# Reordering the products of the seven-product couples, scaling C by rs squared, and other fills around the inverse, in a one-core Hymba block

## The chip, the core and the metric

The kernel runs on one core of a Trainium2 chip. The metric is the device time of one execution in microseconds (us); the median of the runs is compared. Five engines work beside each other and meet at semaphores: PE (TensorE), DVE (VectorE), ACT (ScalarE), POOL (GpSimd), and SP, which here only issues transfers. Each engine takes its instructions in the order of the program.

## What is computed

One layer of a hybrid block over 528 tokens (16 meta tokens and 512 real ones), width 2048:

```
hn = rmsnorm(h_res, norm_in_g)
P  = hn @ w_in                      # 2048 x 8320: lora, r, k, v, g (RWKV-7), B, C, h, gate (short conv)
r, k, v, g, wl, al = token_shift(P[:, :4224])
...                                 # decay and a from two low-rank paths, kk normalised per head
S_t = S_{t-1} diag(w_t) - (S_{t-1} kk_t)(kk_t a_t)^T + v_t k_t^T ;  y_t = S_t r_t   # 16 heads of 64
y_a = (groupnorm(y) + bonus) * silu(g)
y_b = B * conv3(C * h) * silu(g_c)
out = rmsnorm(h_res + concat(y_a, y_b) @ w_out)[16:]
```

All products are fp32-exact: each operand is split into a high and a low fp32r part, and a product is three matmuls (high x high, high x low, low x high).

## The kernel before, in words

The recurrence is done in chunks of 64 tokens: for each of eight pairs of heads `prepare(i)` builds decays, the small Gram products (`gram`) and a 16-wide inverse by DVE; for each two pairs `invert` widens it to 64 by small products `t`, `z` on PE; then `recur` goes through nine chunks for all heads, and the output projection follows (products M, P, Q with seven products in the place of eight).

**The flow.** The input projection is a generator of PE matmuls, `mains()`. Seven column tiles go singly; the other 58 go in 29 couples, numbered here from 0, `couple(p)`, each (t0, t1) one pair of 128-column tiles. A couple takes four of the sixteen 128-row blocks of the input with a second four and the two token halves in a Strassen-like form with seven block products in place of eight; the other eight blocks go straight ("plain", the function `rest`). With 12 matmuls in a form and 24 in a rest, a couple is 7 x 12 + 4 x 24 = 180 matmuls. They gather in four PSUM banks: za, zb, ze, zd (tiles `psa_`, `psb_`, `pse_`, `psd_`, named after t0). za and ze are used several times: ACT copies an interim value (`keep`, L617) or DVE adds it (`add`, L613) before PE goes on adding into the bank.

**The order on PE is written by hand** (`manual_schedule` for PE). All other work on PE, that is the Gram products, the inverse and the recurrence, is placed between matmuls of the flow: `fill(ns)` runs the flow for so many nanoseconds, by 0.46 ns for each column, before the next small product. The table `FW` holds these lengths. The order on DVE, ACT, POOL and SP is set by a scheduler from priorities; `ahead()` gives high priority.

**The weights of a couple.** `sums_of(p + 1)` issues the two loads `ra`, `rb` for couple p + 1 from within couple p, and makes from them on ACT, DVE and POOL the operands of the seven forms: `ah`, `al` (W11, W21), `m` (T1), `bh`, `bl` (T2, W22), `ch`, `cl` (T3, T4). `plain_of(p + 1, 1)` loads `rp` for t1 and splits it: `ph` on ACT, then `pl` on POOL; `plain_of(p, 0)` does so for t0 (`pl` on DVE). All these blocks (128 x 1024) share nine places in SBUF: a block can be written only when the last reader of the block that had its place is done, and a load that must wait for that waits at the head of SP's queue. In the built program the place of `pl` for t1 is that of `ah` of the same couple in most couples (21 of couples 1 to 28), and the place of the raw load `rp` for t1 is that of the couple's own `ah` in 6 couples (3, 9, 13, 14, 19, 20), of `ra` in 14, of `rb` in 6, and of the earlier couple's last `pl` in 2. `bl` follows the earlier couple's `ph` for t1 in 27 of 28.

**h and C.** In the couples (h, C) C is the t1 tile. Both are multiplied by the token scale rs on DVE, then POOL multiplies them (`q_h_C`, L423), ACT and DVE make the convolution `cv`.

Of the kernel before, what the change touches and what calls it, by code (L numbers as in the profile page):

```python
# [13 lines left out]
ALU = mybir.AluOpType  # L14
# [8 lines left out]
META = 16  # L23
L = SEQ + META
# [16 lines left out]


FW = dict(
    evac=34, start=1062, lora=2200, gram=8000, gram_b=13500, gram2=5500, misc=2000, v=2000, vt=1000, solve=24500, solve_first=30000,
    tr=3200, lev=3000, cp=4200, out=1500, begin=20800, p=2900, u=2900, s=4800, last=3700, mix=2600,
)


# [2 lines left out]
W0 = META + HS  # L51
# [32 lines left out]
def hymba_kernel(ctx: ExitStack, tc: tile.TileContext, xt, xtok, front, w_in, w_out, pv, lup, cst, msk, gf, out):  # L84
    nc = tc.nc
# [169 lines left out]
    o = 0  # L255
# [145 lines left out]
    got = {}  # L401

    def use(what, i, q):
        if what == "lora":
            use_lora(q)
        elif what in ("k", "v"):
            t = cq.tile([P, LP], F32, tag=what, name=f"{what}{i}")
            nc.gpsimd.memset(t[:, META:CH], 0.0)
            shifted(q, tile_of[what] + i, t[:, CH:LP], t[:, 0:META])
            got[what, i] = t  # L410
        elif what in ("r", "g"):
            pool, tag = (cq, f"r{i % 2}") if what == "r" else ((cq, "g"), (tp, "cw"))[i % 2]
            t = pool.tile([P, SEQ], F32, tag=tag, name=f"{what}{i}")
            shifted(q, tile_of[what] + i, t)
            if what == "g":
                gate(t, t, f"r{i}")
                later((14000, 8000)[i % 2], lambda: nc.sync.dma_start(gated[i], t))
            got[what, i] = t
        elif what == "C":
            got[what, i] = q  # L420
        elif what == "h":
            u = got["C", i][:, META - 2 : L]
            nc.gpsimd.tensor_tensor(out=u, in0=u, in1=q[:, META - 2 : L], op=ALU.mult)  # L423
            cv = tp.tile([P, SEQ], F32, tag="cw", name=f"cv{i}")
            nc.scalar.activation(cv, u[:, 0:SEQ], AF.Copy, scale=col(V_CW, i))
            for j in (1, 2):
                nc.vector.scalar_tensor_tensor(
                    out=cv, in0=u[:, j : SEQ + j], scalar=col(V_CW, 8 * j + i), in1=cv, op0=ALU.mult, op1=ALU.add
                )
            got[what, i] = cv  # L430
            if i == 0:
                bg = tm("bg")[:, 0:SEQ]
                nc.sync.dma_start(bg, bgd)
                nc.gpsimd.tensor_tensor(out=cv, in0=cv, in1=bg, op=ALU.mult)
                later(9000, lambda: nc.sync.dma_start(mixd[NPAIR], cv))
        elif what == "B":
            b = q[:, META:L]
            if i == 0:
                got[what, i] = tp.tile([P, SEQ], F32, tag="cw", name="cw0")
                nc.scalar.copy(got[what, i], b)  # L440
            else:
                cv = got["h", i]
                o = direct.get(NPAIR + i, cv)
                nc.gpsimd.tensor_tensor(out=o, in0=cv, in1=b, op=ALU.mult)
                if o is cv:
                    later(9000, lambda: nc.sync.dma_start(mixd[NPAIR + i], cv))
        else:
            g = q[:, META:L]
            gate(g, g, f"c{i}")
            cv = got["h", i] if i else got["B", 0]  # L450
            nc.vector.scalar_tensor_tensor(out=cv, in0=cv, scalar=0.5, in1=g, op0=ALU.mult, op1=ALU.mult)
            if i == 0:
                later(5000, lambda: nc.sync.dma_start(bgd, cv))
        ready.add((what, i))
# [118 lines left out]
    def couple(p):  # L573
# [7 lines left out]
        def bank(name):  # L581
            return pm.tile([P, W0], F32, tag="main", name=f"ps{name}_{names[0]}")
# [25 lines left out]
        def part(n, t, c):  # L608
            return qq[:, n, (c, W0)[t] : (W0, L)[t]]

        def add(o, x, z, c):
            with ahead():
                nc.vector.tensor_tensor(out=o, in0=z[:, c:W0], in1=x, op=ALU.add)  # L613

        def keep(o, z, c):
            with ahead():
                nc.scalar.copy(o, z[:, c:W0])  # L617
# [11 lines left out]
        ze = bank("e")  # L629
        yield from form(ze, S1, "T1", META, True)  # L630
        keep(part(0, 1, META), ze, META)
        yield from form(za, S2, "T2", c0)
        keep(part(1, 0, f1), za, f1)
        yield from form(ze, S4, "W22", f1, False, False)
        if p + 1 < len(couples):
            sums_of(p + 1)
        elif chain:
            split_chain()
        yield from form(za, S3, "T3", META)
        add(part(1, 1, META), part(0, 1, META), za, META)  # L640
        yield from rest(ze, 1, 0)
        add(part(1, 0, f1), part(1, 0, f1), ze, f1)
        yield from form(za, X22, "T4", META, False, False)
        zd = bank("d")
        yield from rest(zd, 1, 1, True)
        add(part(1, 1, META), part(1, 1, META), zd, META)
        with ahead():
            q = qq[:, 1, f1:L]
# [2 lines left out]
        if p + 1 < len(couples):  # L651
            plain_of(p + 1, 1)
        yield from rest(zb, 0, 0)
        add(part(0, 0, f0), part(0, 0, f0), zb, f0)
        yield from rest(za, 0, 1)
        with ahead():
            q = qq[:, 0, f0:W0]
            nc.vector.tensor_tensor(out=q, in0=q, in1=rs[:, f0:W0], op=ALU.mult)
            nc.vector.tensor_tensor(out=qq[:, 0, W0:L], in0=za[:, META:W0], in1=rs[:, W0:L], op=ALU.mult)
# [74 lines left out]
    def fill(ns):  # L734
        while ns > 0:
            seen = len(ready)
            t = step()
            if t is None:
                return
            ns -= t  # L740
            if len(ready) > seen:
                ns += FW["evac"]
# [23 lines left out]
    def ahead():  # L766
        return tc.high_priority(offset=AHEAD)
# [262 lines left out]
    def invert(two):  # L1030
# [10 lines left out]
        with ahead():  # L1041
            for q in both:
                nc.vector.transpose(xn[q][:, CH:LP], two[q]["xT"][:, 1:NCH].rearrange("p c s -> p (c s)"))
        fill(FW["tr"])
        z = [pz.tile([P, 2, 4, CH], F32, tag="tz", name=f"t{first}_{e}") for e in range(2)]
        for q in both:
            for k in range(4):
# [519 lines left out]
    z = {}  # L1567
# [159 lines left out]
```

## Time and profile before

| | |
|---|---|
| median of 3 runs | 1140.29 us (1137.03 to 1141.22) |
| the profiled execution | 1144.66 us, of which the span from first to last instruction is 1142.9 us |
| PE busy | 1020.0 us, 89% of the span |
| DVE, ACT, POOL busy | 868.8, 487.8, 265.1 us |
| mean granted TensorE clock | 0.958 |
| matmuls | 9535 |

PE is the engine with the least idle time. Its couples run from 104 us to 971 us of the span, the output projection after that. In the profile's rows a time in brackets is the idle time of the engine ahead of an instruction, and the arrow names what ended it.

### The profile page before, as it was taken

Reading aid. Unit: us, or ns where it says so; the run is one execution under the profiler, and the core shown is the slowest. Engines: PE = TensorE matmul, PEld = TensorE weight load, DVE = VectorE, ACT = ScalarE, POOL = GpSimd, SP = SyncE. Lnnn points to the kernel's source line nnn. Section 1 sums busy time; section 2 is a strip of 40 time slices with the busy share of each in tenths; the row PEclk is TensorE's granted clock in tenths of the full one; section 3 lists DMA queues with packets and bytes.
Section 4 is the critical chain, followed back from the end, with each engine's and each line's share of the span. In section 5 each row is a group of like instructions: output and inputs, shape, how many; then the busy total and the mean of one; then the engine's idle time right before and its main releaser. Section 6 shows DMA issues by size and latency. Waiting matters only on the chain. (4 is left out here: it accounts for less than half of the span.)

```text
span 1142.9 us, 23275 instructions
## 1 busy us (share of the span) xinstructions
PE 1020.0 (89%) x9535; PEld 951.0 (83%) x9535; DVE 868.8 (76%) x1355; ACT 487.8 (43%) x840; POOL 265.1 (23%) x211
## 2 busy tenths in 40 slices
PE   9998889788989878897989897998999898899997
PEld 8897879678979878897988897997898798788886
DVE  7699866558887668976687876657776689999895
ACT  8454433144543344542353443233333333655554
POOL 0122212113312221422232312222222322201101
PEclk9999989888999989999999899999999899999999
DMA  9323626523657322657323566486767376978653
GB/s 305 112 74 94 161 57 175 127 75 99 170 133 185 104 78 80 167 133 193 103 99 94 145 165 166 125 307 226 249 215 223 84 203 200 270 223 257 150 127 147
DMA packets 185563, 180.05 MB, mean 158 GB/s; under 512 B 112240, under 2 KB 141936, under 8 KB 185072
## 3 DMA queue, kind: packets, MB, share of 16 engines
q1 hardware_dynamic: 182864, 169.64, 50.2%
q0 software_dynamic: 2304, 8.39, 4.4%
q8 instruction: 75, 1.23, 0.4%
q10 hardware_dynamic: 288, 0.52, 0.1%
q14 instruction: 32, 0.26, 0.1%
HBM read 139.54 MB, written 38.97 MB: 156 GB/s over the span
## 5 line engine op out<-in xcount | busy, mean ns | idle before, releaser
L556 POOL TENSOR_TENSOR cl<-ra,ch 128x1024 fp32r<-128x1024 f32 x29 | 75.7, 2609 | 299.6 <-ACT ch L554 149.3
L568 ACT CAST ph<-rp 128x1024 fp32r<-128x1024 f32 x58 | 60.6, 1049 | 72.8 <-DMA rp<-in_w_in_dram 72.4
L570 POOL TENSOR_TENSOR pl<-rp,ph 128x1024 fp32r<-128x1024 f32 x29 | 70.8, 2443 | 58.6 <-ACT ph L568 48.1
L570 DVE TENSOR_TENSOR pl<-rp,ph 128x1024 fp32r<-128x1024 f32 x29 | 35.3, 1218 | 30.9 <-ACT ph L568 22.2
L545 ACT CAST m<-rb 128x512 fp32r<-128x512 f32 x29 | 18.0, 621 | 88.5 <-DVE rb L544 61.2
L542 ACT CAST ah<-ra 128x1024 fp32r<-128x1024 f32 x29 | 30.3, 1046 | 47.2 <-DMA ra<-in_w_in_dram 38.0
L1410 ACT CAST o<-x 128x512 fp32r<-128x512 f32 x56 | 34.0, 620 | 31.7 <-PE M L1438 12.9
L1438 PE MATMUL M<-o,S 128*128 128x512 f32 x192 | 46.1, 396 | 0.0
L548 ACT CAST bh<-rb 128x1024 fp32r<-128x1024 f32 x29 | 30.5, 1051 | 32.7 <-DVE rb L547 31.1
L1397 POOL DMA_DIRECT2D x<-in_w_out_dram x16 | 14.3, 895 | 125.9 <-DVE o L1411 100.9
L1438 PEld LDWEIGHTS M<-o,S 128*128 128x128 f32 x192 | 36.1, 188 | 8.7
L1411 DVE TENSOR_TENSOR o<-x,o 128x512 fp32r<-128x512 f32 x56 | 36.6, 685 | 5.6 <-ACT o L1410 4.9
L543 DVE TENSOR_TENSOR al<-ra,ah 128x1024 fp32r<-128x1024 f32 x29 | 35.2, 1215 | 7.1 <-ACT ah L542 7.1
L554 ACT CAST ch<-ra 128x1024 fp32r<-128x1024 f32 x29 | 30.4, 1049 | 15.4 <-DVE ra L549 11.5
L549 DVE TENSOR_TENSOR ra<-ra,rb 128x1024 f32<-128x1024 f32 x29 | 35.7, 1232 | 0.5
L553 DVE TENSOR_TENSOR bl<-rb,bh 128x1024 fp32r<-128x1024 f32 x29 | 35.3, 1216 | 0.1
L1410 ACT CAST o<-wo 128x512 fp32r<-128x512 f32 x42 | 25.0, 620 | 21.6 <-PE M L1438 8.0
L1438 PE MATMUL M<-o,m 128*128 128x512 f32 x108 | 27.3, 411 | 3.6 <-ACT o L1410 2.2
L1411 DVE TENSOR_TENSOR o<-wo,o 128x512 fp32r<-128x512 f32 x42 | 27.6, 686 | 2.4 <-ACT o L1410 2.1
L1438 PEld LDWEIGHTS M<-o,m 128*128 128x128 f32 x108 | 21.3, 198 | 9.0 <-ACT o L1410 2.6
L876 DVE TENSOR_TENSOR gt<-g,gmt 128x512 f32<-128x512 f32 (+1 forms) x48 | 23.9, 546 | 6.3 <-PE g L866 6.2
L546 DVE TENSOR_TENSOR m<-rb,m 128x512 fp32r<-128x512 f32 x29 | 19.9, 685 | 9.6 <-ACT m L545 9.4
(732 smaller groups left out, 4160.0 us busy)
## 6 DMA issues: line engine op xcount, KB each, us to landing
rp<-in_w_in_dram SPq DMA_DIRECT2D x58, 512.0 KB
ct<-opd SPq DMA_DIRECT2D x56, 320.0 KB
ra<-in_w_in_dram SPq DMA_DIRECT2D x29, 512.0 KB
rb<-in_w_in_dram SPq DMA_DIRECT2D x29, 512.0 KB
wo<-in_w_out_dram SPq DMA_DIRECT2D x21, 512.0 KB
opd<-gt SPq DMA_DIRECT2D x16, 576.0 KB
x<-in_w_out_dram POOLq DMA_DIRECT2D x16, 512.0 KB, 5.8
wr<-in_w_in_dram SPq DMA_DIRECT2D x10, 512.0 KB
```

Source lines behind the costliest of these rows:

```text
L542: nc.scalar.copy(ah, a)
L543: nc.vector.tensor_tensor(out=al, in0=a, in1=ah.bitcast(F32), op=ALU.subtract)
L548: nc.scalar.copy(bh, b)
L549: nc.vector.tensor_tensor(out=two, in0=two, in1=b[:, 0:H].unsqueeze(1).to_broadcast([P, 2, H]), op=ALU.subtract)
L553: nc.vector.tensor_tensor(out=bl, in0=b, in1=bh.bitcast(F32), op=ALU.subtract)
L554: nc.scalar.copy(ch, a)
L556: nc.gpsimd.tensor_tensor(out=cl, in0=a, in1=ch.bitcast(F32), op=ALU.subtract)
L568: nc.scalar.copy(h, r)
L570: (nc.gpsimd if n else nc.vector).tensor_tensor(out=lo, in0=r, in1=h.bitcast(F32), op=ALU.subtract)
L1410: nc.scalar.copy(hi, rq)
L1411: nc.vector.tensor_tensor(out=lo, in0=rq, in1=hi.bitcast(F32), op=ALU.subtract)
L1438: nc.tensor.matmul(bank[s], left(prod, jj, m, s), w, start=(jj == 0 and n == 0), stop=(jj == 7 and n == 2))
```

## The change

It does four things. The order of the products in a couple becomes W11, W21, T1, the rest of zd, T2, W22, the rest of ze, T3, the rest of zb, T4, the rest of za; it was W11, W21, T1, T2, W22, T3, the rest of ze, T4, the rest of zd, the rest of zb, the rest of za. `sums_of(p + 1)` stands ahead of W22 (behind it before), and `plain_of(p + 1, 1)` stands behind the add of zd, as before, which is now behind T3. For h, rs multiplies C on POOL (so that C carries rs squared), and h is taken without rs: DVE multiplies it into C, the second token half straight from PSUM. The add of zb gets high priority. And eight entries of `FW` change, one of them new.

```diff
-    ... gram2=5500, misc=2000, v=2000, vt=1000, solve=24500, solve_first=30000,
-    tr=3200, lev=3000, cp=4200, out=1500, ...
+    ... gram2=6500, misc=1500, v=1500, vt=500, solve=24000, solve_first=29500,
+    tr=3200, tr0=6500, lev=3000, cp=4200, out=3000, ...
...
         elif what == "h":
-            u = got["C", i][:, META - 2 : L]
-            nc.gpsimd.tensor_tensor(out=u, in0=u, in1=q[:, META - 2 : L], op=ALU.mult)
+            q, z = q
+            u = got["C", i]
+            nc.gpsimd.tensor_tensor(out=u[:, META - 2 : L], in0=u[:, META - 2 : L], in1=rs[:, META - 2 : L], op=ALU.mult)
+            with ahead():
+                for o, x in ((slice(META - 2, W0), q[:, META - 2 : W0]), (slice(W0, L), z[:, META:W0])):
+                    nc.vector.tensor_tensor(out=u[:, o], in0=u[:, o], in1=x, op=ALU.mult)
...
         ze = bank("e")
         yield from form(ze, S1, "T1", META, True)
         keep(part(0, 1, META), ze, META)
+        zd = bank("d")
+        yield from rest(zd, 1, 1, True)
         yield from form(za, S2, "T2", c0)
         keep(part(1, 0, f1), za, f1)
-        yield from form(ze, S4, "W22", f1, False, False)
         if p + 1 < len(couples):
             sums_of(p + 1)
...
+        yield from form(ze, S4, "W22", f1, False, False)
+        yield from rest(ze, 1, 0)
+        add(part(1, 0, f1), part(1, 0, f1), ze, f1)
         yield from form(za, S3, "T3", META)
         add(part(1, 1, META), part(0, 1, META), za, META)
-        yield from rest(ze, 1, 0)
-        add(part(1, 0, f1), part(1, 0, f1), ze, f1)
-        yield from form(za, X22, "T4", META, False, False)
-        zd = bank("d")
-        yield from rest(zd, 1, 1, True)
         add(part(1, 1, META), part(1, 1, META), zd, META)
...
             plain_of(p + 1, 1)
         yield from rest(zb, 0, 0)
-        add(part(0, 0, f0), part(0, 0, f0), zb, f0)
+        raw0 = t0[0] == "h"
+        with ahead():
+            add(part(0, 0, f0), part(0, 0, f0), zb, f0)
+        yield from form(za, X22, "T4", META, False, False)
         yield from rest(za, 0, 1)
+        if raw0:
+            use(*t0, (qq[:, 0], za))
+            return
...
-        fill(FW["tr"])
+        fill(FW["tr0"])
```

The last lines are in `invert`, ahead of the first products t. The numbers and shapes of the instructions stay the same on every engine; only their order, their operands in the h step, and the places of the weight blocks change.

On PE, in couple 13 (h2 and C2), the first row of each form or rest, before (T4, which reads like T3, stands between the rest of ze and the rest of zd). `psa` to `psd` are the banks za to zd, `ph_1` and `ph_0` the plain weights of t1 and t0:

```order
L589 MATMUL psa_h_5607<-xh,ah_5346 128x258
L589 MATMUL psb_h_5621<-xh,ah_5346 128x258
L589 MATMUL pse_h_5640<-s_114,m_5348 128x256
L589 MATMUL psa_h_5607<-xs_116,bh_5349 128x258
L589 MATMUL pse_h_5640<-xs_116,bh_5349 128x258
L589 MATMUL psa_h_5607<-xh,ch_5350 128x256
L589 MATMUL pse_h_5640<-xh,ph_1_5542 128x258
L589 MATMUL psd_h_5767<-xh,ph_1_5542 128x256
L589 MATMUL psb_h_5621<-xh,ph_0_5636 128x258
L589 MATMUL psa_h_5607<-xh,ph_0_5636 128x256
```

The same now:

```order
L594 MATMUL psa_h_5604<-xh,ah_5358 128x258
L594 MATMUL psb_h_5621<-xh,ah_5358 128x258
L594 MATMUL pse_h_5640<-s_114,m_5360 128x256
L594 MATMUL psd_h_5654<-xh,ph_1_5463 128x256
L594 MATMUL psa_h_5604<-xs_116,bh_5361 128x258
L594 MATMUL pse_h_5640<-xs_116,bh_5361 128x258
L594 MATMUL pse_h_5640<-xh,ph_1_5463 128x258
L594 MATMUL psa_h_5604<-xh,ch_5362 128x256
L594 MATMUL psb_h_5621<-xh,ph_0_5636 128x258
L594 MATMUL psa_h_5604<-xh,ph_0_5636 128x256
```

The first use of `ph_1` has moved from behind six forms to behind three.

On SP, around the load `rp_1` for couple 13, before (`sx`, `xT`, `xo`, `sn`, `sg`, `nd` are transfers of the inverse):

```order
L139 DMA rb_5343<-in_w_in_dram 128x1024
L1002 DMA sx_135<-y_4940 72x16x16
L804 DMA sn_5495<-n_5452 2x9x64
L993 DMA xT_4965<-sx_135 64x9x64
L994 DMA xo_4966<-sx_135 64x4x64
L804 DMA sg_5494<-ga_5372 64x9x64 x2
L804 DMA nd_5500<-sn_5495 72x16
L139 DMA rp_1_5540<-in_w_in_dram 128x1024
L804 DMA d_5499<-sg_5494 72x16x16
```

And now:

```order
L139 DMA rb_5355<-in_w_in_dram 128x1024
L810 DMA opd_74<-vs_5065 32x9x32
L786 DMA lur_6911<-in_lup_dram 128x256
L139 DMA rp_1_5461<-in_w_in_dram 128x1024
L1012 DMA sx_135<-y_5000 72x16x16
L814 DMA sn_5551<-n_5508 2x9x64
L1003 DMA xT_5025<-sx_135 64x9x64
L1004 DMA xo_5026<-sx_135 64x4x64
L814 DMA sg_5550<-ga_5409 64x9x64 x2
```

The load `rp_1` stands ahead of the inverse's transfers now; in both programs it takes the place of the couple's own `ah`.

On PE, in couple 14, around the first products `t` of the third inverse, before:

```order
L589 MATMUL psb_B_5885<-xh,ah_5690 128x256
L589 MATMUL pse_B_5904<-s_114,m_5692 128x256
L1050 MATMUL t_0_5916<-xn_5875,ga_4791 64x64 x2
L1050 MATMUL t_0_5916<-xn_5876,ga_5372 64x64 x2
L589 MATMUL psa_B_5867<-xs_116,bh_5693 128x256
```

And now:

```order
L594 MATMUL psb_B_5881<-xh,ah_5698 128x256
L594 MATMUL pse_B_5900<-s_114,m_5700 128x256
L594 MATMUL psd_B_5918<-xh,ph_1_5779 128x256
L594 MATMUL psa_B_5862<-xs_116,bh_5701 128x256
L594 MATMUL pse_B_5900<-xs_116,bh_5701 128x256
L594 MATMUL pse_B_5900<-xh,ph_1_5779 128x256
L1060 MATMUL t_0_5996<-xn_5911,ga_4853 64x64 x2
L1060 MATMUL t_0_5996<-xn_5912,ga_5409 64x64 x2
```

The products `t` stand behind the rests of zd and most of ze, where they stood in T1. In the second inverse they stand in T2 of couple 9, in the fourth in the rest of zd of couple 20.

The places of the blocks, in the built program now: the raw load `rp` for t1 takes the place of the couple's own `ah` in 8 couples (3, 4, 8, 9, 13, 15, 20, 28), of `ra` in 9 (5, 6, 12, 17, 18, 21, 22, 23, 26), of `rb` in 9 and of the earlier couple's last `pl` in 2 (1, 19). In couples 7, 14 and 16 (among those with `rb`) `ph` takes the place of `ah`. `pl` for t1 takes that of `ah` or `al` in 20. `bl` follows the earlier couple's `ch`, which T4 reads last, in all 28.

More of the change, by code (lines that the diff above doesn't have):

```diff
@@ L43 @@
 FW = dict(
-    evac=34, start=1062, lora=2200, gram=8000, gram_b=13500, gram2=5500, misc=2000, v=2000, vt=1000, solve=24500, solve_first=30000,
-    tr=3200, lev=3000, cp=4200, out=1500, begin=20800, p=2900, u=2900, s=4800, last=3700, mix=2600,
+    evac=34, start=1062, lora=2200, gram=8000, gram_b=13500, gram2=6500, misc=1500, v=1500, vt=500, solve=24000, solve_first=29500,
+    tr=3200, tr0=6500, lev=3000, cp=4200, out=3000, begin=20800, p=2900, u=2900, s=4800, last=3700, mix=2600,
 )
@@ L421, in use @@
         elif what == "h":
-            u = got["C", i][:, META - 2 : L]
-            nc.gpsimd.tensor_tensor(out=u, in0=u, in1=q[:, META - 2 : L], op=ALU.mult)
+            q, z = q
[4 more added lines that the diff above has]
+                    nc.vector.tensor_tensor(out=u[:, o], in0=u[:, o], in1=x, op=ALU.mult)
+            u = u[:, META - 2 : L]
             cv = tp.tile([P, SEQ], F32, tag="cw", name=f"cv{i}")
```

## The prediction

> **What bounds the kernel now.** I read the page's busy rows first, then the clock of the core.
>
> ```profile
> PE 1020.0 (89%) x9535; PEld 951.0 (83%) x9535; DVE 868.8 (76%) x1355; ACT 487.8 (43%) x840; POOL 265.1 (23%) x211
> PEclk9999989888999989999999899999999899999999
> core 0: 1142.9 us, clock 0.958
> ```
>
> PE sets the time: it idles 11% of the span, and the work of PE is not changed. So the question is which idle times go and which come. The mean clock of 0.958 means 2 x 0.042 x 1142.9 = 96 us at half clock, some 48 us of lost cycles: the second thing that can move.
>
> Next the waits of PE, by what ended them (us in total, times, longest):
>
> ```profile
> PE t L1050 <- DVE xn L1043: 15.4, 4, 4.6
> PE tz L754 <- DVE xT L1115: 7.2, 2, 4.6
> PE g L904 <- DVE gt L876: 7.1, 5, 4.2
> PE pse_k L589 <- ACT q_k_v L617: 4.5, 3, 2.4
> ...
> PE psa_v L589 <- DVE q_v_r L613: 3.8, 1, 3.8
> ...
> PE pse_h L589 <- POOL pl L570: 3.2, 3, 1.5
> ...
> PE psa_v L589 <- ACT q_v_r L617: 0.4, 1, 0.4
> PE psa_g L589 <- DVE q_g_g L613: 0.3, 1, 0.3
> ...
> PE psb_B L589 <- DVE pl L570: 0.2, 1, 0.2
> ```
>
> Three groups bear on the change. Around the inverse: 15.4 + 7.2 + 7.1 = 29.7 us. On interim copies and adds of the banks: the 13 rows that end with "ACT q... L617", from 4.5 to 0.4, sum to 24.9, the 5 rows with L613, from 3.8 to 0.3, to 9.2. On weights that are not split yet: the 13 rows that end with ph, pl, al, bl or xl, from 3.2 to 0.2, sum to 23.8. Together 87.6 us: no more idle time than that can be won by this change outside the recurrence.
>
> **The new order against the weights.** A form takes 1.42 us and a rest twice that, by the chain:
>
> ```profile
> 914.08 1.42 PE psa_B L589 x12
> 915.50 2.85 PE psd_B L589 x24
> ```
>
> Before, `ph` and `pl` of t1 are first read after six forms, 6 x 1.42 = 8.5 us into a couple; now after three, 4.3 us, and `pl` two matmuls later. When are they there? The timeline of couple 13 shows it, SP, PE, ACT and POOL (start, us, idle before in brackets):
>
> ```profile
> 506.45 0.36 SPq L139 DMA_DIRECT2D rp<-in_w_in_dram  x1
> ...
> 506.26 0.28 PE L589 MATMUL psb_h<-xh,al 128*128 128x258 f32 x1
> 506.38 1.59 PE L589 MATMUL pse_h<-s,m 128*128 128x256 f32 x12
> 512.97 0.28 PE L589 MATMUL pse_h<-xh,ph 128*128 128x258 f32 x1
> 514.43 0.39 PE L589 MATMUL pse_h<-xh,pl 128*128 128x258 f32 x1 [1.07 <-POOL pl L570]
> ...
> 510.83 1.05 ACT L568 CAST ph<-rp 128x1024 fp32r<-128x1024 f32 x1
> ...
> 512.01 2.37 POOL L570 TENSOR_TENSOR pl<-rp,ph 128x1024 fp32r<-128x1024 f32 x1 [0.36 <-ACT ph L568]
> ```
>
> The load has the place of `ah` and is issued as W21, the last reader of `ah`, ends (506.4). `ph` is done at 511.88, 5.4 us after that, `pl` at 514.38, and PE waited 1.07 us for it even in the old order. In the new one PE is through T1 at 506.38 + 1.42 = 507.80: it waits 4.1 us for `ph`, issues two matmuls (0.24 us), and waits 514.43 - 511.88 - 0.24 = 2.3 us for `pl`. That is 6.4 us in one couple. Eight couples have this place now; in two of them (4 and 15) about 1 us of small products lies in the window: 8 x 6.4 - 2 = 49 us.
>
> Where the load has the place of `ra`, it waits for POOL's `cl`. Couple 21 before, DVE, POOL, SP, ACT and PE:
>
> ```profile
> 723.26 1.22 DVE L553 TENSOR_TENSOR bl<-rb,bh 128x1024 fp32r<-128x1024 f32 x1
> ...
> 725.90 2.39 POOL L556 TENSOR_TENSOR cl<-ra,ch 128x1024 fp32r<-128x1024 f32 x1 [17.15 <-ACT ch L554]
> 734.45 2.38 POOL L570 TENSOR_TENSOR pl<-rp,ph 128x1024 fp32r<-128x1024 f32 x1
> ...
> 728.32 0.33 SPq L139 DMA_DIRECT2D rp<-in_w_in_dram  x1
> ...
> 732.26 1.05 ACT L568 CAST ph<-rp 128x1024 fp32r<-128x1024 f32 x1 [5.91 <-DMA rp<-in_w_in_dram]
> ...
> 732.49 1.59 PE L589 MATMUL pse_h<-s,m 128*128 128x256 f32 x12
> ```
>
> From the issue to the end of `ph` it is 733.31 - 728.32 = 5.0 us. The couple starts at 732.49 - 2.85 = 729.64. `bl` and `ch` now wait for T4 of the couple before, which ends one rest, 2.85 us, ahead of that: at 726.8. Then `bl` to 728.0, `cl` 2.4 to 730.4, the load and `ph` 5.0 to 735.4, `pl` 2.4 to 737.8. PE needs `ph` at 733.9 and `pl` at 735.65: 1.5 + 2.2 = 3.7 us. Six such couples cost 3.5 each, the three in the recurrence (22, 23, 26), with 1 to 2 us of its products in the window, 2 each: 27 us. The rest of the couples: `pl` can't start before W21 ends, so 2.4 us of POOL stand against 1.42 + 0.24 us of PE: 0.8 us, in couples 10, 11 and 27 together 3.5; nothing in 2, 24, 25, where small products cover it. Where `ph` has the place of `ah` (7, 14, 16), 1.05 + 2.4 - 1.66 = 1.8, together 6. Couples 0, 1 and 19, whose load starts with the couple: 5.0 + 2.4 - 4.5 = 3 each, 9. Sum: 49 + 27 + 3.5 + 6 + 9 = 95 us of new waits at the rest of zd. From below the bound is 8 x 5 + 12 x 0.8 = 50 (every other load early), from above 125 (POOL or ACT late by 1 us more in each of the 29 couples). I take 95, for the two worked couples are plain chains of rows.
>
> **What the new order and the fills save.** The interim copies get 4.3 us (a rest and two forms) where they had one form: I take 22 of 24.9 as saved. The adds ahead of T4 have one rest of cover as before, but start behind another add: 3 of 9.2 saved. The waits on weights are taken into the 95: 22 of 23.8 go. The inverse:
>
> ```profile
> 531.92 0.35 SPq L139 DMA_DIRECT2D rp<-in_w_in_dram  x1
> ...
> 532.86 0.60 SPq L993 DMA_DIRECT2D xT<-sx  x1
> ...
> 538.04 0.71 DVE L1043 STREAM_TRANSPOSE xn<-xT 128x512 f32<-128x512 f32 x1 [1.51 <-DMA xT<-sx]
> ...
> 538.81 0.92 PE L1050 MATMUL t<-xn,ga 64*64 64x64 f32 x24 [4.59 <-DVE xn L1043]
> ```
>
> Here the loads of `xT` stood behind an `rp` that waited for W21; `xn` came 6.9 us after that issue. Now `t` stands behind the rest of zd (second to fourth inverse), which waits for the same kind of load, and tr0 is 3.3 us more than tr: all 15.4 go. With out + 1.5 us and a longer couple 6 of 7.2 go, with gram2 + 1 us and the same stretch 5 of 7.1. The fills themselves cost nothing: they move flow that PE has to do anyway, and the flow still reaches past the recurrence.
>
> Sum of the savings: 22 + 3 + 22 + 15 + 6 + 5 = 73 us; between 60 and 87.6.
>
> **h and C** I cost at 0. DVE does two multiplications as before, POOL one; POOL's waits for h's last part,
>
> ```profile
> POOL q_h_C L423 <- DVE q_h_C L659: 54.1, 7, 15.7
> ...
> 733.20 1.29 POOL L444 TENSOR_TENSOR cv<-cv,q_B_gc 128x512 f32<-128x512 f32 x1 [4.91 <-DVE q_B_gc L659]
> ```
>
> become short, but no wait of PE ends in `q_h_C` of POOL or in `cv`. What covers it is the next couple (B, gate), which needs `cv` only at its end. If that cover were gone, POOL's multiplication would cost some 1.3 us (the row of the same shape above) in 8 couples: 10 us at most, of gain.
>
> **The clock.** After a wait the next stretch runs at half clock (columns: us, PE, PEld, DVE, ACT, POOL, PEclk):
>
> ```profile
> 481.60:484.20 2.60, 0.44 (x4) 0.43 (x4) 2.60 (x6) 2.44 (x4) 0.79 (x2) 1.00 0.71 140
> 484.20:487.60 3.40, 3.40 (x28) 3.18 (x28) 3.40 (x5) 1.82 (x3) 2.29 (x1) 0.50 0.24 80
> 487.60:495.00 7.40, 7.38 (x68) 6.67 (x67) 4.60 (x10) 0.00 (x0) 0.00 (x0) 1.00 0.64 172
> ```
>
> A wait of some 2 us costs 3.4 us at half clock, 1.7 us more. About 17 waits of 2 us or more go, about 20 come, and some of these are long enough for two stretches: I add 4 stretches, 6 us; between -29 (all of the old go, none comes) and +15. The Trainium skill, in "TensorE: Matmul & The Clock Gate", section "HAM oscillation", says that idle gaps above about 3.4 us throttle PE; here 2.2 us of idle in 2.6 was enough, so the trace goes further than the rule.
>
> The forecast: 1144.7 (the profiled execution) + 95 - 73 + 6 = 1172.7. The median of the runs is 4.4 below the profiled time: 1168 us, +2.4%.
>
> **Rivals.** *The clock decides the other way (faster).* The 17 long waits that go, in the banks and at the inverse, free their 17 half-clock stretches, 29 us; the new waits come in two pieces of at most 4 us with matmuls between, and throttle nothing. Then 1144.7 + 95 - 73 - 29 - 4.4 = 1133. It decides from 22 us on, 13 stretches more gone than come. For it speaks that the half-clock time is 96 us; against it, that 2.2 us were enough above. The rule of the Trainium skill's page named above, taken at its word, is this rival in part: only the first pieces of the eight long waits (4.1 us) would throttle, 8 x 1.7 = 14 us, which gives 1147.
>
> *Gain and loss balance (no change).* The loads that wait for `ra` and `rb` come early because PE itself stands still, and only the eight `ah` couples and 0.8 us in others are paid: some 70 us against 73: 1144.7 + 70 - 73 - 4.4 = 1137. For it: the waits lengthen every couple, and DVE and ACT catch up. Against it: `bl` and `cl` hang on T4 of the couple before, which moves along with PE.
>
> *The queue of SP makes it worse.* The waiting `rp` now stands ahead of the inverse's store and loads, as at 531.92 above; what is queued behind it are `sx`, `xT`, `sg` and `d`, for which DVE's inverse and then `t` wait. If that comes late in each inverse as at 538.81 (4.6 us) and the late `rp` pushes the next couple's `ra` too, 4 x 4.6 + some 10 us: about 1197. Against it: 20 us of fill lie between these loads and `t`.
>
> **How the numbers follow.** Forecast (net 10 to 45 us, 1150 to 1185): 0.56. SP worse (1185 to 1210): 0.18. The clock (1110 to 1134): 0.15. Balance (1135 to 1146): 0.11. The range 1128 to 1203 leaves out 2 in 10: half of the clock's case and the upper ends. A difference under 0.5%, 5.7 us, can hardly be told from none. So faster 0.15, within 0.5% 0.11, slower 0.74.
>
> **What would show it.** Right: a row "psd <- POOL pl" or "psd <- ACT ph" leads PE's waits, about 95 us in all, with eight couples above 5 us; the rows with L617 and the one of `xn` nearly vanish; the mean clock is at or under 0.958. Wrong: the sum at psd below 60 us, that is, loads issued before W21 ends in most couples; or a clock above 0.965. If psd's waits are there but the time isn't longer, then the savings or the clock were mis-sized.

## The result, and the profile after

The changed kernel takes 1261.35 us (median; 1254.95 to 1263.8) against 1140.76 of the kernel before on the same chip: a ratio of 1.105, interval 1.100 to 1.110. The forecast was 1168 with a range of 1128 to 1203: the sign was right, the size wrong by more than four times, and the time lies outside the range.

The same rows of the page as before (busy time of PE; its clock in 40 slices; span and mean clock of the core):

```profile
PE 1059.6 (84%) x9535; PEld 987.5 (78%) x9535; DVE 856.6 (68%) x1355; ACT 488.3 (39%) x840; POOL 262.0 (21%) x211
PEclk9999798989888898887888889898988988999999
core 0: 1260.3 us, clock 0.906
```

Two things have grown. The same 9535 matmuls keep PE busy for 39.6 us longer, at a lower mean clock: 2 x 0.094 x 1260.3 = 237 us at half clock where it was 96. And PE waits more. The waits of PE (us in total, times, longest), those at psd in full and the first three at psb:

```profile
PE psd_g L594 <- ACT ph L573: 22.5, 4, 10.3
PE psd_B L594 <- ACT ph L573: 18.3, 5, 7.9
PE psd_h L594 <- POOL pl L575: 13.8, 6, 4.7
PE psd_h L594 <- ACT ph L573: 12.4, 5, 4.7
PE psd_r L594 <- POOL pl L575: 11.5, 4, 5.7
PE psd_r L594 <- ACT ph L573: 9.8, 3, 4.2
PE psd_B L594 <- POOL pl L575: 8.8, 5, 1.9
PE psd_k L594 <- POOL pl L575: 8.3, 3, 4.2
PE psd_g L594 <- POOL pl L575: 7.1, 4, 1.9
PE psb_h L594 <- DVE pl L575: 6.7, 2, 6.4
...
PE psd_k L594 <- ACT ph L573: 5.9, 3, 3.3
...
PE psd_v L594 <- POOL pl L575: 5.5, 3, 2.0
...
PE psb_g L594 <- ACT ph L573: 4.8, 1, 4.8
PE psd_v L594 <- ACT ph L573: 4.1, 2, 3.0
...
PE psb_r L594 <- ACT ph L573: 3.6, 1, 3.6
```

The rows at psd, the rest of zd that the change moved forward, sum to 128 us, 73 behind ph and 55 behind pl; there were none before. The interim copies and the t behind xn are gone from the list.

In the table all waits of PE are put into groups. "Weights elsewhere" are the waits at za, zb and ze for ph, pl, al and the like; "banks" those behind the copies and adds of L617 and L613 (L622 and L618 in the changed kernel); "inverse" those of t, tz, z and g. The time is the median, the rest of the row is of the profiled execution.

| kernel | time | PE busy | clock | psd | weights elsewhere | banks | inverse | other |
|---|---|---|---|---|---|---|---|---|
| before | 1140 | 1020.0 | 0.958 | 0 | 23.9 | 34.4 | 32.1 | 25.3 |
| changed | 1261 | 1059.6 | 0.906 | 128.2 | 24.8 | 0.4 | 13.0 | 27.1 |
| new order alone | 1254 | 1056.6 | 0.911 | 120.9 | 14.6 | 2.1 | 31.6 | 20.6 |
| fills, h and C | 1159 | 1021.1 | 0.958 | 0 | 53.8 | 25.5 | 21.4 | 27.7 |
| h and C alone | 1138 | 1019.4 | 0.958 | 0 | 23.2 | 33.6 | 34.1 | 18.7 |
| fills alone | 1158 | 1031.5 | 0.947 | 0 | 50.3 | 23.5 | 22.5 | 23.5 |
| zd one form later | 1234 | 1054.5 | 0.920 | 73.8 | 35.1 | 15.8 | 19.4 | 27.6 |
| zd two forms later | 1207 | 1041.5 | 0.935 | 38.4 | 35.4 | 25.7 | 24.9 | 35.3 |
| T4 earlier | 1248 | 1052.7 | 0.922 | 96.4 | 19.0 | 32.5 | 9.8 | 28.1 |
| filled waits (82.6 us of added matmuls in PE busy) | 1238 | 1107.9 | 0.952 | 51.4 | 21.4 | 2.6 | 12.4 | 26.1 |
| own place | 1202 | 1040.6 | 0.931 | 82.7 | 11.3 | 6.2 | 18.9 | 33.1 |
| high first | 1214 | 1044.3 | 0.930 | 84.2 | 24.6 | 4.7 | 15.0 | 32.2 |
| own place and high first | 1156 | 1028.8 | 0.950 | 50.0 | 11.5 | 8.1 | 17.0 | 32.2 |
| both, zd one form later | 1141 | 1020.2 | 0.952 | 18.2 | 13.6 | 22.6 | 21.1 | 33.2 |
| own place, zd two forms later | 1152 | 1024.0 | 0.952 | 4.1 | 11.0 | 39.7 | 25.5 | 40.2 |
| old order, h and C, own place | 1127 | 1017.5 | 0.958 | 0 | 11.1 | 39.8 | 26.9 | 26.0 |
| the same, new fills | 1130 | 1017.9 | 0.959 | 0 | 12.4 | 50.3 | 17.3 | 25.7 |

Between the two kernels the span grew by 117.4 us: 77.9 of waits (128.2 at psd, less 50.3 elsewhere) and 39.6 of PE busy.

How the wait comes about in couple 13, whose load has the place of its own `ah` (timeline; start, us, idle before):

```profile
558.89 0.33 SPq L139 DMA_DIRECT2D rp<-in_w_in_dram  x1
...
562.75 1.05 ACT L573 CAST ph<-rp 128x1024 fp32r<-128x1024 f32 x1 [1.20 <-DMA rp<-in_w_in_dram]
...
563.85 0.58 PE L594 MATMUL psd_h<-xh,ph 128*128 128x256 f32 x1 [3.44 <-ACT ph L573]
564.09 2.34 POOL L575 TENSOR_TENSOR pl<-rp,ph 128x1024 fp32r<-128x1024 f32 x1
...
566.48 0.58 PE L594 MATMUL psd_h<-xh,pl 128*128 128x256 f32 x1 [1.84 <-POOL pl L575]
```

The load is issued as W21 ends, `ph` is done 4.9 us later, `pl` another 2.6 us later: 5.3 us of waits in this couple, where the prediction had 6.4.

### The profile page after: what moved, and what is told of

Read it like the earlier page. It is cut to its first block, busy times and chain, and to the rows that moved or that the text cites. A ratio compares the mean times of both kernels' runs of the same rounds, so it can differ in the third digit from the quotient of the medians.

```text
span 1260.3 us, 23256 instructions
## 1 busy us (share of the span) xinstructions
PE 1059.6 (84%) x9535; PEld 987.5 (78%) x9535; DVE 856.6 (68%) x1355; ACT 488.3 (39%) x840; POOL 262.0 (21%) x211
## 5 line engine op out<-in xcount | busy, mean ns | idle before, releaser
L561 POOL TENSOR_TENSOR cl<-ra,ch 128x1024 fp32r<-128x1024 f32 x29 | 82.9, 2860 | 332.9 <-ACT ch L559 231.3
L575 DVE TENSOR_TENSOR pl<-rp,ph 128x1024 fp32r<-128x1024 f32 x29 | 35.4, 1219 | 67.3 <-ACT ph L573 65.9
L1420 ACT CAST o<-x 128x512 fp32r<-128x512 f32 x56 | 34.0, 620 | 31.6 <-PE M L1448 13.6
L594 PE MATMUL psd_B<-xh,ph 128*128 128x256 f32 x56 | 21.7, 387 | 18.3 <-ACT ph L573 18.3
L558 DVE TENSOR_TENSOR bl<-rb,bh 128x1024 fp32r<-128x1024 f32 x29 | 35.3, 1218 | 1.1 <-PE ps_gc L349 0.9
L594 PE MATMUL psd_h<-xh,pl 128*128 128x256 f32 x64 | 22.3, 348 | 13.8 <-POOL pl L575 13.8
L594 PE MATMUL psd_h<-xh,ph 128*128 128x256 f32 x64 | 22.3, 349 | 12.4 <-ACT ph L573 12.4
L424 POOL TENSOR_TENSOR q_h_C<-q_h_C,rs 128x514 f32<-128x514 f32 x8 | 12.3, 1541 | 96.0 <-DVE q_h_C L653 80.3
```

The costliest lines, as they stand in the source:

```text
L558: nc.vector.tensor_tensor(out=bl, in0=b, in1=bh.bitcast(F32), op=ALU.subtract)
L561: nc.gpsimd.tensor_tensor(out=cl, in0=a, in1=ch.bitcast(F32), op=ALU.subtract)
L575: (nc.gpsimd if n else nc.vector).tensor_tensor(out=lo, in0=r, in1=h.bitcast(F32), op=ALU.subtract)
L594: nc.tensor.matmul(z[:, cols], ww[:, o], x(xx, k), start=start and k == m == 0, stop=stop and k == count - 1 and m == 2, skip_group_check= ...
L1420: nc.scalar.copy(hi, rq)
```

## The experiments

**Which part of the change loses the time.** Four kernels, each the kernel before with one or two of the parts. The first takes only the order (the lines of `couple` in the change, with neither `ahead` nor the step of h):

```diff
         ze = bank("e")
         yield from form(ze, S1, "T1", META, True)
         keep(part(0, 1, META), ze, META)
+        zd = bank("d")
+        yield from rest(zd, 1, 1, True)
         yield from form(za, S2, "T2", c0)
...
```

> The kernel before with only the new product order in the couples (old fills, h and C as before, no priority for the add of zb). Theory (the order is the whole loss, through the plain weights of t1): 1250 to 1285 us, PE waits at psd of 110 to 150 us against 128 in the changed kernel, mean clock at or under 0.92; the waits of the inverse (t behind xn and the like) are not fewer than before, since the fills are the old ones. Rival (the fills or the h and C step make the places of the weights late, only 3 couples have the load behind their own ah here against 8): the waits at psd are 70 us or less and the time 1190 us or less.

Measured: 1253.9 us, ratio 1.100 (1.098 to 1.103), 121 us of waits at psd, clock 0.911, the inverse's waits unchanged. The theory holds: the order alone costs 114 us, the whole change 121. The number of couples whose load stands behind their own `ah` (3 here, 8 in the changed kernel) hardly matters for the sum. The priority of the add of zb is neither in this kernel nor in the next three: no run shows it by itself.

The second kernel keeps the old order and takes the rest:

```diff
-    gram2=5500, misc=2000, v=2000, vt=1000, solve=24500, solve_first=30000,
+    gram2=6500, misc=1500, v=1500, vt=500, solve=24000, solve_first=29500,
-    tr=3200, ... out=1500,
+    tr=3200, tr0=6500, ... out=3000,
...
+            u = got["C", i]
+            nc.gpsimd.tensor_tensor(out=u[:, META - 2 : L], in0=u[:, META - 2 : L], in1=rs[:, META - 2 : L], op=ALU.mult)
...
```

> The kernel before with the new fills and the new h and C step, but the old product order. Theory (the order is the whole loss): no waits at psd behind ph or pl to speak of (under 10 us), clock 0.95 or more, time 1115 to 1140 us: the fills save up to the 29.7 us of the waits around the inverse. Rival 1 (fills and h with C share in the loss): 1160 us or more. Rival 2 (the fills only shift the waits): 1140 us within 6.

Measured: 1159.0 us, ratio 1.017 (1.015 to 1.019). This is neither the theory's gain nor rival 2, but close to rival 1: some 19 us are lost here too. The inverse wins 11 us and the banks 9, and the waits on weights take 30. So the two pieces were run apart. h and C alone, the second part of the diff above:

> The kernel before with the new h and C step alone (old order, old fills). Theory (the 19 us that the fills and this step lost together came from the fills, which shift the places of the weights): 1140 us within 6, waits on weights about 24 us as before. Rival (the step itself loses: the new multiplications on DVE and POOL stand ahead of the splits of weights): 1150 us or more, with waits on weights of 40 us or more.

Measured: 1137.7 us, ratio 0.998 (0.996 to 1.000): nothing, as the theory said. The fills alone, the first part:

> The kernel before with the new fills alone. Theory (the fills carry the loss): 1150 to 1165 us, waits of the inverse under 22 us against 32, waits on weights 45 us or more against 24. Rival (the h and C step carries it): 1115 to 1140 us.

Measured: 1157.5 us, ratio 1.016 (1.012 to 1.020). The inverse's waits fell to 22.5 us, the waits on weights rose from 24 to 50. In the built program of this kernel the load of t1's plain weights takes the place of the couple's own `ah` in 10 couples, where the kernel before has 6. The rows of its waits that carry it:

```profile
PE pse_h L589 <- POOL pl L570: 6.3, 4, 2.9
PE psb_h L589 <- DVE pl L570: 5.3, 2, 2.8
PE psb_B L589 <- DVE pl L570: 4.9, 3, 2.7
...
PE pse_B L589 <- POOL pl L570: 4.2, 3, 2.8
```

The fills move no work to another engine, and still they cost. What they move are the moments at which the blocks are made, and so who inherits whose place; how much of the loss that is, the kernels with another place show (below). In this kernel's profiled run little of the loss is waits in sum: of the 15.7 us that its span is longer, 4 are waits (26 more on weights, 22 fewer at the inverse, the banks and elsewhere), and 11.5 are PE busy, at a clock of 0.947. In the kernel with h and C as well it is the other way round, 13 us of waits and 1 of PE busy.

**Lead of the plain weights.** The changed kernel with the rest of zd one form later:

```diff
-        zd = bank("d")
-        yield from rest(zd, 1, 1, True)
         yield from form(za, S2, "T2", c0)
         keep(part(1, 0, f1), za, f1)
+        zd = bank("d")
+        yield from rest(zd, 1, 1, True)
```

> The changed kernel with the rest of zd one form later: W11, W21, T1, T2, rest of zd, W22, rest of ze and so on. Theory (the plain weights come at a time set by W21 and by T4 of the couple before, so each 1.42 us of PE work ahead of them is 1.42 us less wait): in the 25 couples that waited the waits at psd fall by 25 x 1.42 = 36 us from 128 to about 92, PE busy falls by some 10 to 15 us through the clock, time 1205 to 1220 us. Rival (the loads move along with the order, or other waits come): waits at psd 115 us or more and time above 1240 us.

Measured: 1234.0 us, ratio to before 1.083 (1.080 to 1.085). The waits at psd fell by 54 us, more than the 36 expected, but 15 came back at the banks and 10 at other weights, and PE busy fell by 5 us alone; so the time fell by 27 where 41 to 56 was expected. And two forms later, with the same two lines behind W22:

> The changed kernel with the rest of zd two forms later: W11, W21, T1, T2, W22, rest of zd, rest of ze, T3 and so on. Theory (as for one form): the waits at psd fall by 20 to 25 couples x 2.84 us, to about 60 to 70 us, the clock rises to about 0.945; the interim copy of ze is again covered by one form alone (some 5 to 8 us of waits come back); time 1155 to 1180 us. Rival (the clock and the waits don't follow the lead of the plain weights): above 1220 us.

Measured: 1207.4 us, ratio 1.058 (1.053 to 1.063): again the waits at psd fall (38 us left, below what was expected), and again the time falls by less than they do (54 us against 90, from the changed kernel). It lies between the theory's range and the rival's: the lead sets the waits at psd, but the time it frees is partly waited for in the next place, at the banks, the inverse and the rest of zb.

**The chain from the couple before.** T4 ahead of the rest of zb:

```diff
+        yield from form(za, X22, "T4", META, False, False)
         yield from rest(zb, 0, 0)
...
-        yield from form(za, X22, "T4", META, False, False)
         yield from rest(za, 0, 1)
```

> The changed kernel with T4 put ahead of the rest of zb (T3, T4, rest of zb, rest of za). T4 is the last reader of ch and cl, whose places bl of the next couple takes; it now ends a rest (2.85 us) earlier against the next couple. Theory (in the couples whose load has the place of ra or rb, the chain T4, bl, ch, cl sets the load): the waits at psd fall by up to 17 x 2.85 = 48 us, from 128 to 80 to 100; T4 now waits for the adds behind T3 (29 x about 1 us at bank za); time 1205 to 1240 us. Rival (the couple's own W21 sets the load nearly everywhere): waits at psd 115 us or more, time 1260 us or more, since the waits of T4 are added.

Measured: 1247.7 us, ratio 1.093 (1.091 to 1.095). The waits at psd are 96 us, 32 less, and T4 waits 32.5 us for the adds. The theory holds on the waits; the time, 14 us less, lies just above its range, since the new wait costs as much as the old one did, but for the clock.

**The clock.** 24 matmuls of no use in each couple, where PE would wait:

```diff
         zd = bank("d")
+        for k in range(24):
+            nc.tensor.matmul(zd[:, META:W0], xh[:, 0, META : META + P], moving(xh, 0, 1, META), start=True, stop=True)
+            yield 0
         yield from rest(zd, 1, 1, True)
```

> The changed kernel with 24 matmuls of 128x256 put ahead of the rest of zd in each couple; they read the input alone, and the rest overwrites what they leave in zd, so that nothing else changes. They take 29 x 2.85 = 83 us at full clock. Of the waits at psd 61 us stay by the sums of the couples (what is over 2.85 us in each), 67 go. Theory (the 40 us that PE busy gained are half clock behind these waits): 1260 + 83 - 67 - 20 to 35 = 1240 to 1256 us, fewer than 25 stretches of half clock against 37. Rival (the half clock has other sources): 1270 us or more, mean clock still 0.91 or less.

Measured: 1238.0 us, ratio to before 1.088 (1.083 to 1.093), 23 us less than the changed kernel, with 696 matmuls more. Its page:

```profile
PE 1107.9 (90%) x10231; PEld 1041.4 (85%) x10231; DVE 850.4 (69%) x1355; ACT 487.7 (40%) x840; POOL 261.0 (21%) x211
...
core 0: 1229.8 us, clock 0.952
```

Without the 82.6 us of the added matmuls PE is busy for 1025.3 us: 34 of the 39.6 us are back. The waits at psd left 51 us, where 61 was expected. There are 26 stretches of half clock against 37, where the theory had fewer than 25, and 118 us in place of 236. The mean clock of this kernel's four runs was 0.942 to 0.952, and the profile is of the one at 0.952, so 34 us is the most that came back. Most of the loss of clock was the waits at psd. In couple 11 it shows directly. First the changed kernel, then this one (columns: us, PE, PEld, DVE, ACT, POOL, PEclk, DMA share, GB/s); the rest of zd begins at 482.73 in the former and at 470.37 in the latter:

```profile
478.00:481.00 3.00, 1.70 (x15) 1.49 (x13) 3.00 (x7) 0.72 (x1) 2.02 (x1) 1.00 0.69 209
481.00:484.00 3.00, 0.80 (x2) 0.50 (x2) 2.40 (x4) 2.27 (x3) 1.25 (x1) 0.62 0.37 141
484.00:488.00 4.00, 2.83 (x13) 2.84 (x14) 0.00 (x0) 0.00 (x0) 1.11 (x1) 0.50 0.41 125
488.00:492.00 4.00, 3.98 (x29) 3.17 (x29) 1.62 (x3) 2.27 (x5) 0.00 (x0) 0.93 0.11 26
```

```profile
466.00:469.00 3.00, 3.00 (x27) 3.00 (x26) 2.08 (x5) 0.00 (x0) 0.00 (x0) 1.00 0.77 238
469.00:472.00 3.00, 1.87 (x15) 1.57 (x13) 1.04 (x1) 2.74 (x4) 1.61 (x1) 1.00 0.79 279
472.00:476.00 4.00, 3.21 (x19) 2.85 (x19) 3.68 (x4) 0.13 (x1) 0.74 (x1) 0.74 0.04 10
```

Two waits with two matmuls between (3.03 and 1.64 us) brought 6.8 us of half clock, from 481.7 to 488.5; it set in 2.0 us after the first wait began (479.70). The one wait of 1.93 us that is left in the other kernel brought 3.4 us, from 473.9.

**The load's place and the length of pl.** First a place of its own for the raw load of t1 (the one that `ph` of t0 had):

```diff
-        r = raw_unit(f"rp{p}_{n}")
+        r = tp.tile([P, 1024], F32, tag="ph", name=f"rp{p}_{n}") if n else raw_unit(f"rp{p}_{n}")
...
-            h = block_of(f"ph{p}_{n}") if n else tp.tile([P, 1024], F32R, tag="ph", name=f"ph{p}_{n}")
+            h = block_of(f"ph{p}_{n}")
```

> The changed kernel with an SBUF place of its own for the raw load of the plain weights of t1 (the place that ph of t0 had; ph of t0 now shares the nine places). Theory (the load that waits for a place is what makes the weights late): the load lands before the couple starts, ph then waits for its place and pl behind cl on POOL; the waits at psd fall from 128 to 25 to 50 us, the clock to 0.94 or more, time 1140 to 1180 us. Rival (the chain T4, bl, ch, cl on DVE, ACT and POOL holds pl anyway): waits at psd of 90 us or more, time 1220 us or more.

Measured: 1202.0 us, ratio 1.056 (1.054 to 1.058). The waits at psd behind ph fell from 73 to 23 us, those behind pl stayed (60 us). Half the theory, then: 83 us are left where 25 to 50 was expected. The late load was one cause, and there is a second one at pl. (Of the 23 us behind ph, 9.4 are in couple 1, whose load was not late; more on that below.) Two were open: pl is held by its place or by `cl` in POOL's queue, or it is simply longer (2.4 us) than what PE has to do meanwhile (two matmuls, 0.24 us). So the next kernel changes only that, the order within a rest:

```diff
-            for k in range(count):
-                o = slice(k * P, (k + 1) * P)
-                for m, (ww, xx) in enumerate(((hi, 0), (hi, 1), (lo, 0))):
+            three = list(enumerate(((hi, 0), (hi, 1), (lo, 0))))
+            order = [(k, *t) for k in range(count) for t in three]
+            if count > NS:
+                order.sort(key=lambda t: t[1] == 2)
+            for k, m, (ww, xx) in order:
```

> The changed kernel with the matmuls of each rest in another order: the 16 that read ph first, then the 8 that read pl (before: two of ph, one of pl, and so on). The places of the blocks at the rest of zd are as in the changed kernel but for one couple. The 16 take 1.90 us where the two take 0.24. Theory (55 us of the waits at psd are pl's 2.4 us on POOL against 0.24 us of PE): the rows psd behind pl fall by 25 x 1.66 = 41 us to about 14, those behind ph stay at about 73, the clock rises somewhat, time 1200 to 1220 us. Rival (pl is held by its place or by cl on POOL and not by its own length, so PE meets it later but as late): the rows behind pl stay above 40 us, time above 1240 us.

Measured: 1214.0 us, ratio 1.065 (1.061 to 1.068). The rows behind pl at psd, in full:

```profile
PE psd_r L598 <- POOL pl L575: 3.2, 2, 2.9
PE psd_h L598 <- POOL pl L575: 2.9, 5, 1.7
PE psd_v L598 <- POOL pl L575: 0.3, 1, 0.3
PE psd_B L598 <- POOL pl L575: 0.3, 1, 0.3
PE psd_g L598 <- POOL pl L575: 0.3, 1, 0.3
```

7 us of 55 are left, those behind ph are 77. The theory holds in the main: in the changed kernel pl's waits are mostly its own length. The trace of that kernel says the same: in 19 of the 25 couples with such a wait POOL begins pl within 0.33 us of the end of ph, and these waits sum to 34.5 us. In the other six (0, 3, 5, 7, 9 and 16), 20.5 us, POOL begins it 1.1 to 4.2 us after ph, so there its queue has a share. Both edits together:

> The changed kernel with both the place of its own and the rests with the high products first. Alone they left 83 us (23 behind ph, 60 behind pl) and 84 us (77 and 7) of waits at psd. Theory (two separate causes, the load's place and the length of pl): about 23 us behind ph and 60 - 21 x 1.66 = 25 us behind pl, 35 to 55 us in all; time 1145 to 1170 us, clock 0.945 or more. Rival (pl of the kernel with the place of its own is held by cl in POOL's queue, not by its length): 60 us or more behind pl and ph, time 1180 us or more.

Measured: 1155.5 us, ratio 1.013 (1.008 to 1.017), 50 us at psd, 23 behind ph and 27 behind pl, clock 0.950. The two causes are separate: against the changed kernel the time falls by 59 and by 47 us alone, and by 106 together.

**Is there a better version?** The place of its own with the rest of zd two forms later:

> The changed kernel with the rest of zd two forms later and the place of its own. Theory: of the 74 us of waits on weights that the two forms alone left, at least 45 go, the clock rises to 0.95; time 1150 to 1175 us. Rival (what is left is not the load's place, but the chain over POOL): above 1190 us.

Measured: 1151.7 us, ratio 1.009 (1.007 to 1.012), as the theory had it: 4 us left at psd, and 40 at the banks. With the high products first and one form later:

> As the kernel with both, and the rest of zd one form later (W11, W21, T1, T2, rest of zd, W22, rest of ze, T3, rest of zb, T4, rest of za). Theory (1.42 us more of lead take the rest of the waits at psd, and the interim copy of ze keeps the cover of the rest of zd): waits at psd 15 us or less, at the banks 10 to 20 us against 40 in the old order with the place of its own; time 1110 to 1135 us, about as fast as the old order with the place of its own (1127) or faster. Rival (waits elsewhere, at the banks, the inverse and the recurrence, keep the new order behind): 1140 us or more.

Measured: 1141.0 us, ratio 0.999 (0.997 to 1.002). This is the rival: the waits at psd (18 us) and banks (23) are about as expected, but the recurrence and the rest take 33 us, and the new order, cured of most of its waits, is just as fast as the old one. The same place in the old order, with the new h and C step:

> The kernel before with the new h and C step and with the place of its own for the raw load of the plain weights of t1. Theory (also in the old order a part of the waits on weights, 23 us, comes from the shared places): waits on weights 10 us or less, time 1115 to 1130 us. Rival (those waits are of POOL and of t0's weights, which now share the places): 1138 us within 8.

Measured: 1126.7 us, ratio 0.985 (0.981 to 0.990): the lowest median of all, with 11 us of waits on weights where there were 23. And the new fills on top:

> The old order with the new fills, the new h and C step and the place of its own for the raw load. Theory (the new fills lose only by moving the places of the weights: 54 us of waits on weights against 24, 10 us less at the inverse): with the place of its own the waits on weights are 15 us or less, so time 1105 to 1125 us, below the kernel before. Rival (the fills lose in themselves, by the clock or by the recurrence): 1140 us or more.

Measured: 1130.4 us, ratio 0.991 (0.989 to 0.993). Neither: the loss of the fills is gone (1130 against 1159), the waits on weights are 12 us and the inverse has 10 us less, but the banks take 10 us more. With the new h and C step the fills cost 21 us in the shared places (1159 against 1138) and 4 with the place of its own (1130 against 1127). So they lose mainly by the places of the weights, and without that they win nothing. The place of its own was not tried with the fills alone.

## Why the prediction was wrong, by its steps

**The mechanism was right.** The plain weights come too late for the new order, `ph` after its load and `pl` after `ph`, and the waits stand at psd in the couples named. What failed were the sizes of three terms:

| term | predicted (bounds) | measured |
|---|---|---|
| new waits at psd | +95 (50 to 125) | +128.2 |
| waits saved elsewhere | -73 (60 to 87.6) | -50.3 |
| clock (growth of PE busy) | +6 (-29 to +15) | +39.6 |
| sum | +28 | +117.5 |

**New waits.** By the groups of the prediction, summed over the waits of each couple:

| group | couples | predicted | measured |
|---|---|---|---|
| load in the place of `ah` | 3, 4, 8, 9, 13, 15, 20, 28 | 49 | 49.4 |
| load in the place of `ra` | 5, 6, 12, 17, 18, 21, 22, 23, 26 | 27 | 29.6 |
| load in the place of `rb` | 2, 10, 11, 24, 25, 27 | 3.5 | 12.2 |
| `ph` in the place of `ah` | 7, 14, 16 | 6 | 21.0 |
| load with the start of the couple | 0, 1, 19 | 9 | 15.9 |

The sums of the first two groups, worked out as a chain of rows, came out; their couples did so less well. In the first group six couples lie below the prediction (4.1 to 5.9 us), and couples 3 and 28 far above it (9.9 and 9.6). In the second they run from 0 to 9.2 us where 2 to 3.5 was predicted. That the sums agree so closely is in part luck.

The step that failed is the price of the other groups. Those with `rb` and with `ph` in the place of `ah` were costed by the length of the conversions alone, as if the load came early. (Three couples at 0.8 us were also put down as 3.5 us; it is 2.4.) The load comes late there too. Couple 11, load in the place of `rb`, which starts at 475.07:

```profile
476.53 1.23 DVE L558 TENSOR_TENSOR bl<-rb,bh 128x1024 fp32r<-128x1024 f32 x1
...
477.78 0.84 SPq L139 DMA_DIRECT2D rp<-in_w_in_dram  x2
...
481.63 1.04 ACT L573 CAST ph<-rp 128x1024 fp32r<-128x1024 f32 x1 [1.59 <-DMA rp<-in_w_in_dram]
482.73 0.58 PE L594 MATMUL psd_v<-xh,ph 128*128 128x256 f32 x1 [3.03 <-ACT ph L573]
482.75 2.36 POOL L575 TENSOR_TENSOR pl<-rp,ph 128x1024 fp32r<-128x1024 f32 x1 [2.73 <-ACT ph L573]
485.17 0.58 PE L594 MATMUL psd_v<-xh,pl 128*128 128x256 f32 x1 [1.64 <-POOL pl L575]
```

`rb` is free when `bl` is made, at 477.76, 2.7 us into the couple, and the load goes out at once. From the issue to the end of `ph` it is 4.9 us, and T1 ends 4.6 us into the couple: it would have had to go out before the couple starts. That happens in couples 0 and 5 alone; in the other 27 the load goes out 0.2 to 6.6 us after the start, whichever block it follows. The prediction also let each conversion begin as soon as its input was there. In couple 1, of the last group, the load goes out 0.24 us after the start, and still PE has its longest wait:

```profile
145.88 0.67 ACT L853 COPY bk<-bk 64x576 f32<-64x576 f32 x1 [2.05 <-DVE bk L852]
146.57 1.04 ACT L573 CAST ph<-rp 128x1024 fp32r<-128x1024 f32 x1
...
147.67 0.58 PE L594 MATMUL psd_g<-xh,ph 128*128 128x256 f32 x1 [10.29 <-ACT ph L573]
```

ACT begins `ph` 13.7 us after the issue, in couple 11 3.9 us after it: copies of the Gram step that wait for DVE stand ahead of it. The load's place is not the cause, for in the kernel with the place of its own this couple still waits 9.4 us behind ph. In couples 3, 7 and 16 POOL begins `pl` 4.2, 2.8 and 2.1 us after `ph` is done, behind `cl` and other steps, and PE waits 5.7, 4.7 and 4.2 us for it.

So the kernel with 3 loads behind `ah` waits 121 us, much like the one with 8. The rival of a balance, with some 70 us, rested on the same error. The bound of 125 was set as 1 us more in each couple, from no row.

**Savings.** The banks gave 34.0 us (25 predicted), the inverse 19.1 (26 predicted: `t` all of its 15, `tz` 4.5 of its 7, and `g` nothing). The term that failed is the 22 of 23.8 us of waits on weights: they were taken as going over into the new waits at psd, but as much came back elsewhere, 24.8 us, most of it at psb. Couple 13 shows how the longest of these waits comes about:

```profile
575.98 1.05 ACT L573 CAST ph<-rp 128x1024 fp32r<-128x1024 f32 x1 [3.00 <-DMA rp<-in_w_in_dram]
...
576.97 0.43 DVE L618 TENSOR_TENSOR q_h_C<-pse_h,q_h_C 128x258 f32<-128x258 f32 x1 [13.60 <-PE pse_h L594]
...
583.61 1.21 DVE L575 TENSOR_TENSOR pl<-rp,ph 128x1024 fp32r<-128x1024 f32 x1
...
584.88 0.58 PE L594 MATMUL psb_h<-xh,pl 128*128 128x258 f32 x1 [6.38 <-DVE pl L575]
```

DVE stands 13.6 us at the head of its queue for the add of ze, which PE reaches late, among other things because it waited 5.3 us itself; the inverse's steps and then `pl` for t0 are queued behind, and PE waits 6.4 us for that `pl`. The Trainium skill says in "TensorE: Matmul & The Clock Gate", section "Architectural detail: the array is 16× 32×32, not 1× 128×128", that the queues of ACT and DVE are strictly first in, first out; this row agrees. The raw load for t0 was late as well, behind the inverse's transfers on SP. So the rival of SP's queue was right on the place of these transfers, but its price did not fall on `t`, which waits for nothing now; it fell on the rest of zb. The next two waits at psb (4.8 us in couple 12, 3.6 in couple 3) end at ph on ACT; their cause was not followed up.

**Clock.** The prediction weighed some 17 stretches that go against some 20 that come. 37 stand where 22 stood, and they are longer: 236 us in place of 95.5, 6.4 us each in place of 4.3. A couple waits twice, for ph and for pl, and in couple 11 the two waits gave one stretch of 6.8 us. The kernel with the filled waits shows, in its profiled run, that 34 of the 39.6 us belong to the waits. The rival in which the clock is gained back had the sign wrong.

**The range** reached to 1203, though the term's own bounds, taken together, gave 1144.7 + 125 - 60 + 15 - 4.4 = 1220. A wait, its clock and the savings it eats are one cause, so they miss together, and the ends should have been added.

**h and C at nothing** was right (ratio 0.998). **The fills at nothing** was wrong: alone they cost 17 us, mainly by the places of the weights. In the changed kernel that price is partly in the order's already: 114 + 17 - 2 is 129, and 121 was measured.

## What to carry to other kernels

When an instruction on the bounding engine is moved forward, work out the lead of its operands for every place that they can come to stand in, not only for the worst: with nine shared places nearly every load waited for some reader of the same couple. Ask, too, what stands ahead of the conversion in its engine's queue. Split a wait into the load and the conversion behind it; most of the first went away with a place of its own (73 to 23 us), the second by putting the products that need no conversion first (55 to 7 us). And a wait of 2 to 4 us on TensorE is to be costed with its clock: here 128 us of waits cost some 34 us more.

## What the runs showed of the hardware

That 696 more matmuls make a kernel 23 us faster was not expected at this size. The clock fell at shorter waits than the Trainium skill gives: its page "TensorE: Matmul & The Clock Gate", section "HAM oscillation — how this bites in real kernels", names idle gaps of more than about 3.4 us, while the changed kernel has 15 single waits of that length and 37 stretches of half clock. In couple 11 half clock set in 2.0 us into a wait of 3.03 us. What decides for a single wait of about 2 us whether the clock falls was not settled.

It stays open, too, why the waits of the recurrence and what is put under "other" rise from 25 to some 33 us in several of the kernels in the new order.
